# Splitting every second weight group of an input projection one group ahead, from buffers of its own, and holding the first down weights ready

## The chip, the cores and the metric

The kernel runs on one core of a Trainium2 chip. The metric is the device time of one execution in microseconds (us), lower is better. The chip's engines named here are TensorE (PE, with its weight loads PEld), VectorE (DVE), ScalarE (ACT), GpSimd (POOL) and SyncE (SP), on whose queue all the transfers of this kernel are issued in order.

## The reference

One step of a decoder layer for a prompt of 1024 tokens and a sample group of 8 x 8 tokens, which together are 1088 rows of width 1024. All matmuls are float32.

```python
h = x + 0.5 * SwiGLU_1(rms(x))                        # w_gate, w_up, w_down, D_FF = 2816
z = rms(h) @ W_in   # -> [q_A | k_A | v_A | q_B | k_B | v_B | gate_A | gate_B], 2048 + 2048 columns
# A: sliding-window attention, 8 q heads / 2 kv heads, window 128, a learned sink per head
# B: dilated attention, 12 q heads in 3 groups (window, dilation) = (128,1), (512,4), (2048,16),
#    4 kv heads; the sample tokens attend to 2048 cached positions (cache_dil_k, cache_dil_v)
h = h + W_out(sigmoid(gate_A) * (o_A @ W_a) + sigmoid(gate_B) * (o_B @ W_b))
h = h + CrossAttn_4heads(rms(h), memory keys / values)
h = h + 0.5 * SwiGLU_2(rms(h))
y = rms_final(h)
```

## The kernel before, in words

Float32 products are made of three matmuls in a rounded format: both operands are split into a high part and the rest (`xh`, `xl`; `whi`, `wlo`), and high x high, high x low and low x high are summed (`mm3`, L319 to L322).

Weights come through the class `Weights` (L50 to L101). `load` (L61) issues a transfer from HBM into a raw buffer, `split` (L69) makes `whi` on ScalarE (L77) and `wlo` on VectorE (L78) in a ring of split buffers, and `prefetch` (L82) runs splits up to `ring` entries and loads up to `ahead` more ones ahead of use, but not past `limit`. `get` takes the next split entry, `done` frees it and prefetches. The main object `ws` has 4 split buffers and 2 raw ones and walks one list, `entries`, through the whole program: down weights of the first FFN (72), the 16 of the input projection, gate weights and so on. An entry is up to 128 x 1024 numbers, 0.5 MB.

The stages are these.

- First FFN: gate and up products by `products` (L403, loop over `j` in 1 .. NJ-1, NJ = 11) with weight buffers of their own, then `down` (L494): three chunks of tokens, for each 8 output blocks `mo` of three entries. Its results go through `xscr`, and are normalized and split into `xh` and `xl` (L719 to L729; `xa` is chunk 0 loaded back at L721).
- Input projection (L804 to L820): four column groups of 512 (`GRP`, L232), for each 9 tiles of tokens with 24 matmuls (L815 to L817) into PSUM banks pS, pf or pO; ScalarE evacuates (`z_out`, L784, L787), POOL applies the rotary embedding (L778 to L782), and SP stores z (`zscr`, L792; `o_dil_k`, `o_dil_v`, L802).
- Decode attention B for the sample tokens (L830 to L984), in pools opened in the middle of the projection's life by `early`: in pool `db`, twice (two halves `p_`), QP is cleared on POOL (L871), 8 key blocks `krb` are loaded into two buffers (L888), transposed on PE (L892), split into KHb and KLb (L316, L317) and multiplied (L320 to L322), then masked (`ttr`, L761) and put through a softmax (L904 to L919); P is transposed (L933) and split. Then 24 value entries (`cache_dil_v`, 0.5 MB each) come through a `Weights` of three raw and three split buffers, one split after the other, with 26 matmuls for each three (L957 to L971).
- Gate units (`gate`, L1099): 24 matmuls each on gate columns of `w_in`, for 16 blocks x 3 token chunks; `tg` (L1111) takes the result. The program puts them between other work as filler.
- Decode attention A, prompt attention, output projection, memory attention, second FFN.

A scheduler orders the instructions of each engine from the tile dependencies, from buffers and their addresses, and from priorities (`early` raises one). Each engine then works its list in order.

Of the kernel before, what the change touches and what calls it, by code (L numbers as in the profile page):

```python
# [27 lines left out]
RAWB = 2  # L28
# [21 lines left out]
class Weights:  # L50
# [3 lines left out]
    def __init__(self, nc, rawp, ringp, entries, ring, ahead, size=1024):  # L54
        self.nc, self.rawp, self.ringp, self.entries = nc, rawp, ringp, entries
        self.ring, self.ahead, self.size = ring, ahead, size
        self.raw, self.parts = {}, {}
        self.n_raw = self.n_split = self.used = self.taken = 0
        self.limit = len(entries)

    def load(self):  # L61
        n = self.n_raw
# [19 lines left out]
    def prefetch(self):  # L82
        total = self.limit
        while self.n_split < min(self.used + self.ring, total):
            self.split()
        while self.n_raw < min(self.n_split + self.ahead, total):
            self.load()

    def get(self, name):
# [15 lines left out]
NJ = MF // 2  # L105
# [85 lines left out]
def trunk(ctx, tc, A, O, dbg=None):  # L191
    nc = tc.nc
# [3 lines left out]
    def pool(name, bufs=1, space=None, side=None):  # L196
        kw = {} if space is None else {"space": space}
        return tc.tile_pool(name=name, bufs=bufs, side=side, reuse_waits="tile", **kw)
# [15 lines left out]
    entries = []  # L214
# [4 lines left out]
    def kview(n):  # L219
        return lambda t: t[:, :].rearrange("p (k c) -> p k c", k=n)  # L220
# [11 lines left out]
    GRP = [(1024, 512), (512, 512), (1536, 512), (0, 512)]  # L232
    ffn_entries("ffn1")
    w_in = A["w_in"].rearrange("(k p) f -> p k f", p=128)
    for gi, (c0, cw) in enumerate(GRP):
        for kk in range(4):
            entries.append((f"in{gi}.{kk}", [(kview(2), w_in[:, 2 * kk:2 * kk + 2, c0:c0 + cw])], 1024))
    gate_entries = []
    for m in range(16):
        gate_entries.append((f"gt{m}", [(kview(8), w_in[:, :, 2048 + m * 128:2048 + (m + 1) * 128])], 1024))  # L240
# [71 lines left out]
    ws = Weights(nc, rawp, ringp, entries, RING, RAWB)  # L312
# [38 lines left out]
    def norm_stats(psp, ss, j0=0, j1=9):  # L351
        finish_rstd(rcol[:, j0:j1], col_sums(psp, ss, range(j0, j1)), j1 - j0)
# [50 lines left out]
    def products(ops, quads, psA, tp, vp, hook):  # L403

        def bank(tag):
            return psA.tile([128, 512], F32, name="p" + tag, tag=tag, bufs=2)

        def rhs(s, nm):  # L410
            return [a[:, :].rearrange("p (k c) -> p k c", k=4) for a in ops.t[s, nm]]

        def mms(p, w, x, first, last):
            wh, wl = (a.rearrange("p (k f) -> p k f", k=4) for a in w)
            for k in range(4):
                PE.matmul(p, wh[:, k], x[0][:, k], start=first and k == 0, stop=False, skip_group_check=True)  # L416
                PE.matmul(p, wh[:, k], x[1][:, k], start=False, stop=False, skip_group_check=True)  # L417
                PE.matmul(p, wl[:, k], x[0][:, k], start=False, stop=last and k == 3, skip_group_check=True)  # L418

        def out(j, s, v):  # L420
            SP.dma_start(out=hscr[j][s][:, :, :].rearrange("p q c -> p (q c)"), in_=v)

        def new(p, nm):
            return p.tile([128, 4 * H], F32, name=nm, tag=nm, bufs=2)


        w0 = {}
        for s in range(2):
            t, v = new(tp, "tg"), new(vp, "tv")
            pairs = [((0, g), (2, g)) for g in range(2)] + [((1, g), (3, g)) for g in range(2)]  # L430
            if s == 0:
                groups = [(0, 0), (0, 1), (2, 0), (2, 1), (1, 0), (1, 1), (3, 0), (3, 1)]
            else:
                groups = [(0, 0), (1, 0), (0, 1), (1, 1), (2, 0), (3, 0), (2, 1), (3, 1)]
            for n, (c, g) in enumerate(groups):
                b, a1, a2, b1, b2 = PLAIN[c]
                for a in (a1, a2):
                    if (g, a) not in w0:
                        w0[g, a] = quads.get(a)
                p = bank(b)[:, :H]  # L440
                mms(p, w0[g, a1], rhs(s, b1), True, False)
                mms(p, w0[g, a2], rhs(s, b2), False, True)
                cs = slice(c * H, (c + 1) * H)
                if g == 0:
                    S.activation(t[:, cs], p, AF.Silu)
                else:
                    V.tensor_tensor(v[:, cs], t[:, cs], p, op=ALU.mult)
                if s and n % 2:
                    quads.done(2)
                hook(s, n)  # L450
            out(0, s, v)


        for j in range(1, NJ):
            ts = [new(tp, "tg") for _ in range(2)]
            for g in range(2):
                vs = ts if g == 0 else [new(vp, "tv") for _ in range(2)]
                ps = {}
                for i, (b, a, nm) in enumerate(PROD):
                    w = quads.get(a)  # L460
                    for s in range(2):
                        first = (b, s) not in ps
                        if first:
                            ps[b, s] = bank(b)[:, :H]
                        mms(ps[b, s], w, rhs(s, nm), first, True)
                    for s in range(2):
                        p, t = ps[b, s], ts[s]
                        c11, c12, c21, c22 = (vs[s][:, c * H:(c + 1) * H] for c in range(4))
                        if i == 0:
                            S.activation(c22, p, AF.Copy)  # L470
                        elif i == 1:
                            V.tensor_tensor(c12, c22, p, op=ALU.add)
                        elif i == 2:
                            if g == 0:
                                S.activation(c11, p, AF.Silu)
                            else:
                                V.tensor_tensor(c11, t[:, 0:H], p, op=ALU.mult)
                        elif i == 3:
                            V.tensor_tensor(c21, c22, p, op=ALU.add)
                        elif i == 4:  # L480
                            V.tensor_tensor(c22, c21, p, op=ALU.add)
                        elif i == 5:
                            V.tensor_tensor(c21, c21, p, op=ALU.subtract)
                        else:
                            V.tensor_tensor(c12, c12, p, op=ALU.add)
                            o = slice(H, 4 * H)
                            if g == 0:
                                S.activation(vs[s][:, o], vs[s][:, o], AF.Silu)
                            else:
                                V.tensor_tensor(vs[s][:, o], t[:, o], vs[s][:, o], op=ALU.mult)  # L490
                                out(j, s, vs[s])
                    quads.done()

    def down(pre, resid, after, stack, stackr):  # L494

# [64 lines left out]
    with ExitStack() as ph:  # L560
# [96 lines left out]
        def hook1(s, n):  # L657
# [37 lines left out]
            if s == 1 and n == 7:  # L695
                ops.split(1, "T3")
                ops.split(1, "T4")

        products(ops, quads, psA, tp, tp, hook1)
        ws.limit = ws.index("ffn2d0.0.0")  # L700
        pq.close()
        sqp = ph.enter_context(pool("sqp0", 1))
# [35 lines left out]
    with ExitStack() as ph:  # L738
# [63 lines left out]
                    SP.dma_start(out=o, in_=z[:rows, j * 256:(j + 1) * 256])  # L802

        p_m1 = tc.cur_priority  # L804
        norm_stats(Stats(), ss)
        for gi in range(4):
            parts = [ws.get(f"in{gi}.{kk}") for kk in range(4)]
            for n, t in enumerate((5, 6, 7, 8, 3, 4, 0, 1, 2)):
                rows = 128 if t < 8 else 64
                p = bank(psS, "pS") if gi == 0 and n % 5 < 3 else bank(psf, "pf") if n % 5 % 2 else bank(pso, "pO")  # L810
                tok = slice(t * 128, t * 128 + rows)
                for k in range(KD):
                    wh, wl = parts[k // 2]
                    cs_ = slice((k % 2) * 512, (k % 2) * 512 + 512)
                    PE.matmul(p[:rows], xh[:, k, tok], wh[:, cs_], start=(k == 0), stop=False)  # L815
                    PE.matmul(p[:rows], xh[:, k, tok], wl[:, cs_], start=False, stop=False)
                    PE.matmul(p[:rows], xl[:, k, tok], wh[:, cs_], start=False, stop=(k == KD - 1))  # L817
                    if n == 8 and k % 2:
                        ws.done()
                z_out(gi, t, rows, p)  # L820
        p_m1e = tc.cur_priority
        bcast_rstd(Stats())
        if stop("proj"):
# [3 lines left out]
        with early(p_m1), ExitStack() as sp_:  # L827
# [21 lines left out]
            with ExitStack() as sb_:  # L849
# [3 lines left out]
                with pool("db") as db:  # L853
                    maskB = db.tile([128, 832], F32, name="maskB")
                    SP.dma_start(out=maskB, in_=A["c_maskb"])
                    for p_ in range(2):
                        pk = bank(pst, "pT")
                        PE.transpose(pk[:, 0:64], zs[:, 1536 + p_ * 128:1664 + p_ * 128], ident[:64, :64])
                        for g in range(3):
                            c0 = 768 + g * 256 + p_ * 128  # L860
# [92 lines left out]
                for b in range(8):  # L953
# [21 lines left out]
                    for p_ in range(2):  # L975
                        c0 = (p_ * 8 + b) * 16
# [371 lines left out]
    with ExitStack() as ph:  # L1348
# [11 lines left out]
        with ExitStack() as p3:  # L1360
# [5 lines left out]
            for c in range(3):  # L1366
                c0, n = CH[c]
# [98 lines left out]
        for c in range(3):  # L1466
# [4 lines left out]
            c0, n = CH[c]  # L1471
# [23 lines left out]
    with ExitStack() as ph:  # L1495
# [20 lines left out]
        for wi, nm in enumerate(("w_mem_k", "w_mem_v")):  # L1516
            parts = [ws.get(f"{nm}{kk}") for kk in range(4)]
# [230 lines left out]
    with ExitStack() as ph:  # L1748
# [38 lines left out]
                ops2.split(1, "T4")  # L1787

        products(ops2, quads, psA, tp, tp, hook2)
        ws.limit = len(entries)  # L1790
        pq.close()
        xqs.close()
# [134 lines left out]
```

## Time and profile before

| | before |
|---|---|
| median of 3 runs | 2630.32 us (2623.37 to 2632.29) |
| profiled execution, time / span | 2627.26 / 2625.5 us |
| busy: PE, DVE, ACT, POOL | 95%, 57%, 40%, 14% |
| mean granted clock of PE | 0.98 |
| input projection, first matmul | 794.29 us |
| third gate unit, first matmul | 1084.62 us |

The profile is one execution. "Busy" is the share of the span; a wait row gives the time that an engine stood idle before an instruction of a line, and whose instruction ended it. A DMA issue stands on SP at the time of its issue, not of its landing. Lines are those of the kernel before; the changed kernel's line numbers are 1 higher from L61 on, 6 higher around the projection's stores and 13 higher behind the projection.

### The profile page before, as it was taken

To read this page: it belongs to the slowest core of one execution; us is meant where nothing else is said; L and a number is where in the kernel's file an instruction comes from. 1 tells how busy PE (TensorE), PEld (TensorE's weight loads), DVE (VectorE), ACT (ScalarE), POOL (GpSimd) and SP (SyncE) were. 2 spreads that over 40 slices of the span, in tenths; PEclk is the share of its full clock that TensorE was granted. 3 is DMA by queue.
4 is the path that set the end of the run, shared out by engine and by line. 5 is a ranking of instruction groups with operands and counts; after the bars stand their busy time and mean duration, and the time that the engine had idled before them with its cause. 6 is when DMAs were issued, how large, how long until landed. Compare 5 with 4: busy or idle time off the path is not lost.

```text
span 2625.5 us, 43436 instructions
## 1 busy us (share of the span) xinstructions
PE 2505.5 (95%) x16981; PEld 2401.8 (91%) x16981; DVE 1488.2 (57%) x3015; ACT 1049.4 (40%) x1890; POOL 361.2 (14%) x453
## 2 busy tenths in 40 slices
PE   5999999999999999899899899999799999999998
PEld 5999999989997787899798899898799999989998
DVE  6755555554334324468677644475865555656543
ACT  6422223244334234357666424364432223234432
POOL 0000000001114722100234232102200000001111
PEclk7999999999999999999899999999899999999999
DMA  6222222297655745533211462525522222257753
GB/s 190 79 87 70 83 70 87 80 277 214 191 156 178 255 154 161 184 94 93 73 59 60 127 221 72 178 77 171 147 80 69 83 70 87 67 183 204 218 159 91
DMA packets 437197, 341.28 MB, mean 130 GB/s; under 512 B 35088, under 2 KB 407424, under 8 KB 436992
## 3 DMA queue, kind: packets, MB, share of 16 engines
q1 hardware_dynamic: 436992, 338.51, 41.9%
q8 instruction: 133, 2.18, 0.3%
q14 instruction: 72, 0.59, 0.1%
HBM read 267.47 MB, written 70.98 MB: 129 GB/s over the span
## 4 chain that ended last, share of the span: by engine, by line
PE 81%; DMA 7%; DVE 5%; ACT 3%; issue 2%; POOL 1%; SPq 1%; POOLq 0%; ACTq 0%; DVEq 0%
PE pd L322 6%; PE pd L321 6%; PE pd L320 6%; PE pX L418 3%; PE pX L416 3%; PE pX L417 3%; PE pY L416 3%; PE pY L418 3%; PE pY L417 3%; PE pZ L418 3%; PE pZ L416 3%; PE pZ L417 3%; PE pb L320 2%; PE pb L321 2%; PE pb L322 2%
## 5 line engine op out<-in xcount | busy, mean ns | idle before, releaser
L78 DVE TENSOR_TENSOR wlo<-wraw,whi 128x1024 fp32r<-128x1024 f32 (+2 forms) x248 | 284.4, 1151 | 293.1 <-ACT whi L77 291.7
L77 ACT ACTIVATE whi<-wraw 128x1024 fp32r<-128x1024 f32 (+2 forms) x248 | 242.8, 982 | 378.7 <-DMA wraw<-ffn_w_down 149.5
L368 POOL TENSOR_TENSOR ss<-ss,sq 128x384 f32<-128x384 f32 (+2 forms) x98 | 127.4, 1300 | 1728.7 <-ACT sq L367 1720.8
L320 PE MATMUL pd<-h,whi 128*128 128x384 f32 (+1 forms) x1056 | 347.0, 330 | 10.2 <-ACT whi L77 6.9
L321 PE MATMUL pd<-h,whi 128*128 128x384 f32 (+1 forms) x1056 | 347.1, 329 | 2.3 <-DVE h L317 2.3
L322 PE MATMUL pd<-h,wlo 128*128 128x384 f32 (+1 forms) x1056 | 347.6, 329 | 1.6 <-DVE wlo L78 1.6
L163 ACT ACTIVATE whi<-rA 128x512 fp32r<-128x512 f32 x256 | 151.9, 625 | 387.0 <-issue 174.7
L320 PEld LDWEIGHTS pd<-h,whi 128*128 128x128 f32 x1056 | 199.5, 189 | 12.4 <-ACT whi L77 7.8
L321 PEld LDWEIGHTS pd<-h,whi 128*128 128x128 f32 x1056 | 199.7, 189 | 3.5 <-DVE h L317 3.5
L322 PEld LDWEIGHTS pd<-h,wlo 128*128 128x128 f32 x1056 | 199.8, 189 | 2.7 <-DVE wlo L78 2.7
L164 DVE TENSOR_TENSOR wlo<-rA,whi 128x512 fp32r<-128x512 f32 x256 | 169.3, 688 | 33.1 <-ACT whi L163 27.7
L320 PE MATMUL pf<-xh,whi 128*128 128x384 f32 (+1 forms) x336 | 114.7, 341 | 6.6 <-DVE tg L1112 6.5
L322 PE MATMUL pf<-xh,wlo 128*128 128x384 f32 (+1 forms) x336 | 113.5, 338 | 0.0
L321 PE MATMUL pf<-xl,whi 128*128 128x384 f32 (+1 forms) x336 | 112.1, 334 | 0.0
L416 PE MATMUL pX<-B11h,whi 128*128 128x272 f32 x352 | 103.0, 293 | 9.5 <-DVE xo L1587 5.9
L418 PE MATMUL pX<-B11h,wlo 128*128 128x272 f32 x352 | 102.6, 291 | 0.0
L417 PE MATMUL pX<-B11l,whi 128*128 128x272 f32 x352 | 102.1, 291 | 0.0
L418 PE MATMUL pX<-B21h,wlo 128*128 128x272 f32 x352 | 101.6, 289 | 0.0
L416 PE MATMUL pX<-B21h,whi 128*128 128x272 f32 x352 | 101.6, 289 | 0.0
L418 PE MATMUL pZ<-B22h,wlo 128*128 128x272 f32 x352 | 101.5, 288 | 0.0
L416 PE MATMUL pZ<-B22h,whi 128*128 128x272 f32 x352 | 101.3, 288 | 0.0
L417 PE MATMUL pX<-B21l,whi 128*128 128x272 f32 x352 | 101.1, 287 | 0.0
(582 smaller groups left out, 7508.3 us busy)
## 6 DMA issues: line engine op xcount, KB each, us to landing
wraw<-ffn_w_down SPq DMA_DIRECT2D x96, 512.0 KB
hscr<-tv SPq DMA_DIRECT2D x44, 544.0 KB
rA<-ffn_w_gate SPq DMA_DIRECT2D x88, 256.0 KB
rA<-ffn_w_up SPq DMA_DIRECT2D x88, 256.0 KB
wraw<-ffn_w_down SPq DMA_DIRECT2D x48, 384.0 KB
hst<-hscr SPq DMA_DIRECT2D x44, 384.0 KB
wraw<-w_in SPq DMA_DIRECT2D x32, 512.0 KB
wraw<-cache_dil_v SPq DMA_DIRECT2D x24, 512.0 KB
```

Of the source, the lines that this page charges most:

```text
L77: self.nc.scalar.activation(hi[:, :w], t[:, :w], AF.Copy)
L78: self.nc.vector.tensor_tensor(lo[:, :w], t[:, :w], _b(hi[:, :w]), op=ALU.subtract)
L163: self.nc.scalar.activation(hi, r[q], AF.Copy)
L164: V.tensor_tensor(lo, r[q], _b(hi), op=ALU.subtract)
L320: PE.matmul(out, lh, rh, start=first, stop=False)
L321: PE.matmul(out, lh, rl, start=False, stop=False)
L322: return PE.matmul(out, ll, rh, start=False, stop=last)
L368: G.tensor_tensor(ss[:, d0:d0 + n], ss[:, d0:d0 + n], q[:, :n], op=ALU.add)
L416: PE.matmul(p, wh[:, k], x[0][:, k], start=first and k == 0, stop=False, skip_group_check=True)
L417: PE.matmul(p, wh[:, k], x[1][:, k], start=False, stop=False, skip_group_check=True)
L418: PE.matmul(p, wl[:, k], x[0][:, k], start=False, stop=last and k == 3, skip_group_check=True)
```

## The change

Two edits. In `products`, at j = NJ - 3, `ws.held` is set to the number of raw buffers and `prefetch` is called, so that the first two down weights may be loaded although `limit` still holds the splits back; `held` is set back to 0 behind the gate and up part. In the input projection the column groups 1 and 3 come from a list `in_entries` of their own, through a `Weights` object `wi` with three raw buffers (pool `iraw`) and a ring of four (`iring`) on the right side of SBUF, whose prefetch is first called behind the second tile of group 0; the pools are closed behind the projection. Groups 0 and 2 still come through `ws`.

```diff
--- before.py
+++ after.py
@@ -57,6 +57,7 @@
         self.raw, self.parts = {}, {}
         self.n_raw = self.n_split = self.used = self.taken = 0
         self.limit = len(entries)
+        self.held = 0
 
     def load(self):
         n = self.n_raw
@@ -83,7 +84,7 @@
         total = self.limit
         while self.n_split < min(self.used + self.ring, total):
             self.split()
-        while self.n_raw < min(self.n_split + self.ahead, total):
+        while self.n_raw < min(self.n_split + self.ahead, total + self.held):
             self.load()
 
     def get(self, name):
@@ -232,9 +233,10 @@
     GRP = [(1024, 512), (512, 512), (1536, 512), (0, 512)]
     ffn_entries("ffn1")
     w_in = A["w_in"].rearrange("(k p) f -> p k f", p=128)
+    in_entries = []
     for gi, (c0, cw) in enumerate(GRP):
         for kk in range(4):
-            entries.append((f"in{gi}.{kk}", [(kview(2), w_in[:, 2 * kk:2 * kk + 2, c0:c0 + cw])], 1024))
+            (in_entries if gi % 2 else entries).append((f"in{gi}.{kk}", [(kview(2), w_in[:, 2 * kk:2 * kk + 2, c0:c0 + cw])], 1024))
     gate_entries = []
     for m in range(16):
         gate_entries.append((f"gt{m}", [(kview(8), w_in[:, :, 2048 + m * 128:2048 + (m + 1) * 128])], 1024))
@@ -490,6 +492,9 @@
                                 V.tensor_tensor(vs[s][:, o], t[:, o], vs[s][:, o], op=ALU.mult)
                                 out(j, s, vs[s])
                     quads.done()
+            if j == NJ - 3:
+                ws.held = RAWB
+                ws.prefetch()
 
     def down(pre, resid, after, stack, stackr):
 
@@ -697,6 +702,7 @@
                 ops.split(1, "T4")
 
         products(ops, quads, psA, tp, tp, hook1)
+        ws.held = 0
         ws.limit = ws.index("ffn2d0.0.0")
         pq.close()
         sqp = ph.enter_context(pool("sqp0", 1))
@@ -802,9 +808,13 @@
                     SP.dma_start(out=o, in_=z[:rows, j * 256:(j + 1) * 256])
 
         p_m1 = tc.cur_priority
+        ix = ExitStack()
+        wi = Weights(nc, ix.enter_context(pool("iraw", 3, side="right")),
+                     ix.enter_context(pool("iring", 4, side="right")), in_entries, 4, 3)
         norm_stats(Stats(), ss)
         for gi in range(4):
-            parts = [ws.get(f"in{gi}.{kk}") for kk in range(4)]
+            wg = wi if gi % 2 else ws
+            parts = [wg.get(f"in{gi}.{kk}") for kk in range(4)]
             for n, t in enumerate((5, 6, 7, 8, 3, 4, 0, 1, 2)):
                 rows = 128 if t < 8 else 64
                 p = bank(psS, "pS") if gi == 0 and n % 5 < 3 else bank(psf, "pf") if n % 5 % 2 else bank(pso, "pO")
@@ -816,8 +826,11 @@
                     PE.matmul(p[:rows], xh[:, k, tok], wl[:, cs_], start=False, stop=False)
                     PE.matmul(p[:rows], xl[:, k, tok], wh[:, cs_], start=False, stop=(k == KD - 1))
                     if n == 8 and k % 2:
-                        ws.done()
+                        wg.done()
                 z_out(gi, t, rows, p)
+                if gi == 0 and n == 1:
+                    wi.prefetch()
+        ix.close()
         p_m1e = tc.cur_priority
         bcast_rstd(Stats())
         if stop("proj"):
@@ -1787,6 +1800,7 @@
                 ops2.split(1, "T4")
 
         products(ops2, quads, psA, tp, tp, hook2)
+        ws.held = 0
         ws.limit = len(entries)
         pq.close()
         xqs.close()
```

In the built programs `iring` takes bytes 114,656 to 147,424 of each partition and `iraw` 147,424 to 159,712. In both programs pool `db` has its krb buffers at 112,896 to 116,992, KHb at 116,992 to 121,088 and KLb at 121,088 to 125,184.

The three places below are where instructions move. Rows are those of the built programs: line, operation, tiles, shape, and how many alike stand in a row.

SyncE's queue in the last third of the first FFN's down part, before (L721 loads `xa`, L708 stores the result of an output block):

```order
L65 DMA wraw<-ffn_w_down 128x6x128
L65 DMA wraw<-ffn_w_down 128x8x128 x2
L721 DMA xa<-xscr_90 128x8x384
L708 DMA xscr_90<-xr 128x256
L708 DMA xscr_90<-xr 128x64
L65 DMA wraw<-ffn_w_down 128x6x128
L65 DMA wraw<-ffn_w_down 128x8x128 x2
L708 DMA xscr_90<-xr 128x384
```

The same place now:

```order
L66 DMA wraw<-ffn_w_down 128x8x128 x2
L727 DMA xa<-xscr_90 128x8x384
L66 DMA wraw<-w_in 128x2x512
L714 DMA xscr_90<-xr 128x256
L714 DMA xscr_90<-xr 128x64
L66 DMA wraw<-w_in 128x2x512
L66 DMA wraw<-ffn_w_down 128x6x128
L66 DMA wraw<-w_in 128x2x512
L66 DMA wraw<-ffn_w_down 128x8x128
L714 DMA xscr_90<-xr 128x384
L66 DMA wraw<-ffn_w_down 128x8x128
```

Three loads of w_in stand among the down weights, behind the load of `xa`. The first two loads of down weights of the whole program stand four rows apart within the first 50 rows of this queue in both programs.

ScalarE at the end of group 0 of the projection, before (`z` rows evacuate a tile each):

```order
L787 ACTIVATE z<-pS,rcol 128x512 x3
L787 ACTIVATE zs<-pf,rcol 64x512
L787 ACTIVATE z<-pO,rcol 128x512
L787 ACTIVATE z<-pS,rcol 128x512 x3
L77 ACTIVATE whi<-wraw 128x1024 x2
L787 ACTIVATE z<-pf,rcol 128x512
L349 ACTIVATE rbc<-pT 128x512 x2
L349 ACTIVATE rbc<-pT 128x128
L77 ACTIVATE whi<-wraw 128x1024 x2
```

The same place now:

```order
L78 ACTIVATE whi<-wraw 128x1024 x3
L793 ACTIVATE z<-pS,rcol 128x512 x3
L78 ACTIVATE whi<-wraw 128x1024
L793 ACTIVATE zs<-pf,rcol 64x512
L793 ACTIVATE z<-pO,rcol 128x512
L793 ACTIVATE z<-pS,rcol 128x512 x3
L78 ACTIVATE whi<-wraw 128x1024 x2
L793 ACTIVATE z<-pf,rcol 128x512
```

The splits of group 1 moved from the end of group 0 to its first tiles, and those of group 2 follow inside group 0 as well.

SyncE's queue in the last group of the projection, before (L888 loads cached keys):

```order
L888 DMA krb<-cache_dil_k 128x4x128 x2
L802 DMA o_dil_v_p<-z 128x256
L792 DMA zscr<-z 128x512
L802 DMA o_dil_k_p<-z 128x256
L888 DMA krb<-cache_dil_k 128x4x128
L65 DMA wraw<-w_in 128x2x512 x2
L802 DMA o_dil_v_p<-z 128x256
L888 DMA krb<-cache_dil_k 128x4x128
L65 DMA wraw<-w_in 128x8x128
L792 DMA zscr<-z 128x512
L888 DMA krb<-cache_dil_k 128x4x128
L802 DMA o_dil_k_p<-z 128x256
```

The same place now, and what follows up to the values:

```order
L808 DMA o_dil_v_p<-z 128x256
L798 DMA zscr<-z 128x512
L808 DMA o_dil_k_p<-z 128x256
L66 DMA wraw<-w_in 128x8x128 x2
L798 DMA zscr<-z 128x512 x7
L868 DMA maskB<-c_maskb 128x832
L901 DMA krb<-cache_dil_k 128x4x128 x2
L798 DMA zscr<-z 128x512
L901 DMA krb<-cache_dil_k 128x4x128 x14
L960 DMA selB<-c_selb 64x32
L66 DMA wraw<-cache_dil_v 128x1024 x24
```

All 16 key loads moved from between the stores of group 2 and 3 to behind them, and the 24 value loads follow in one piece. On PE, in the same way, the matmuls of the decode attention moved from between the projection's to behind its last tile and behind 38 matmuls of the first two gate units; behind the decode attention the two lists of PE are the same.

## Rows read from the trace of the kernel before

**Rows 1.** Busy time, share of the span and instructions of each engine
```profile
PE 2505.5 (95%) x16981; PEld 2401.8 (91%) x16981; DVE 1488.2 (57%) x3015; ACT 1049.4 (40%) x1890; POOL 361.2 (14%) x453
```

**Rows 2.** Timeline of PE: start, us, instruction [idle before, what ended it]
```profile
794.29 0.50 PE L815 MATMUL pS<-whi,xh 128*128 128x512 f32 x1 [1.02 <-ACT xh L727]
...
1084.62 0.63 PE L320 MATMUL pf<-xh,whi 128*128 128x320 f32 x1 [3.64 <-DVE tg L1112]
```

**Rows 3.** Windows: us, busy (x instructions) by engine, granted clock, DMA share, GB/s
```profile
862.00:893.00 31.00, 30.77 (x133) 23.09 (x131) 8.85 (x14) 3.72 (x6) 24.42 (x47) 1.00 0.88 290
...
1018.00:1070.00 52.00, 52.00 (x317) 44.00 (x316) 29.35 (x27) 27.34 (x30) 9.43 (x16) 1.00 0.77 250
1070.00:1085.00 15.00, 8.63 (x49) 6.83 (x49) 6.49 (x10) 4.64 (x8) 2.38 (x3) 0.75 0.36 112
sum 293.00, PE 277.64 PEld 220.85 DVE 114.91 ACT 105.20 POOL 119.00; mean PE 34.71 PEld 27.61 DVE 14.36 ACT 13.15 POOL 14.87
```

**Rows 4.** Waits of PE in 846 to 862 and 893 to 935: us, times, longest
```profile
PE pO L816 <- DVE wlo L78: 5.4, 3, 3.2
PE pO L815 <- ACT whi L77: 0.4, 1, 0.4
...
PE pO L815 <- ACT whi L77: 0.9, 1, 0.9
PE pO L815 <- ACT z L787: 0.7, 1, 0.7
PE pO L816 <- DVE wlo L78: 0.5, 1, 0.5
```

**Rows 5.** Timeline of SP's queue, the first load of down weights
```profile
66.55 0.39 SPq L65 DMA_DIRECT2D wraw<-ffn_w_down  x1
```

**Rows 6.** Timelines of SP and ACT, a down load and its split
```profile
707.65 0.38 SPq L65 DMA_DIRECT2D wraw<-ffn_w_down  x1
...
715.40 0.85 ACT L77 ACTIVATE whi<-wraw 128x768 fp32r<-128x768 f32 x1 [5.94 <-DMA wraw<-ffn_w_down]
```

**Rows 7.** Key load, its transposes, QP's clearing (timelines); a 0.5 MB load (chain)
```profile
953.63 0.55 SPq L888 DMA_DIRECT2D krb<-cache_dil_k  x1
...
959.09 0.62 PE L892 MATMUL pT<-ident,krb 128*128 128x128 f32 x4
...
965.78 4.07 POOL L871 MEMSET QP<- 128x1152 f32 x4 [0.92 <-PE pS L321]
...
1667.03 3.87 DMA wraw<-w_mem_q
```

**Rows 8.** Softmax: timelines of DVE and ACT, and ACT's wait in it
```profile
1001.78 0.69 DVE L761 CUSTOM_DVE_ANT_0 PB<-pS,maskB 128x512 f32<-128x512 f32 x1 [3.98 <-PE pS L322]
...
ACT PT L316 <- PE pT L933: 2.9, 1, 2.9
...
1014.17 1.05 ACT L77 ACTIVATE whi<-wraw 128x1024 fp32r<-128x1024 f32 x1
```

**Rows 9.** Timeline of SP's queue: value loads 4, 7, 10 (same buffer) and 24
```profile
1016.50 0.33 SPq L65 DMA_DIRECT2D wraw<-cache_dil_v  x1
...
1025.60 0.33 SPq L65 DMA_DIRECT2D wraw<-cache_dil_v  x1
...
1031.93 0.33 SPq L65 DMA_DIRECT2D wraw<-cache_dil_v  x1
...
1070.25 0.33 SPq L65 DMA_DIRECT2D wraw<-cache_dil_v  x1
```

**Rows 10.** Chain of waits: two value matmuls, from their start to the next one's
```profile
1055.61 0.12 PE pS L970
...
1078.81 0.21 PE pS L971
```

## The prediction

> **What bounds the kernel now.** I read the page's busy shares first: TensorE (PE) is busy in 95% of the span [rows 1], so a change gains where PE waits and loses where PE is made to wait. Then I took the stretch that the edits touch, from the first matmul of the input projection at 794.29 to the first matmul of the third gate unit at 1084.62 [rows 2]. Behind the decode attention the two programs issue the same work in the same order, so I let a shift of that second mark pass on to the end. The windows show two kinds of work between the marks. Where PE does projection matmuls alone, it is busy in 30.77 of 31.00 us with 133 of them: 31.00 / 133 = 0.233 us each. Where the decode attention's values arrive, PE is also full (52.00 of 52.00 us) while the DMA queues are 77% busy at 250 GB/s: the transfers lie under projection and gate matmuls. In the last 15 us that cover has run out, and PE is busy for only 8.63 [rows 3]. The reader is to see that the decode attention is work at the pace of transfers, and that the projection hides it.
>
> PE's waits at the borders of the column groups are 5.4 + 0.4 in 846 to 862 and 0.9 + 0.5 in 893 to 935, 7.2 us in all, each on a split of w_in; a wait of 0.7 there is for a PSUM bank [rows 4]. That is all the change can save in this stretch.
>
> **The change, part by part.** *First down weights.* The first of the two loads is already issued at 66.55 in the trace of before [rows 5], and the second stands four places behind it on SyncE's queue (SP) in both programs; the scheduler had hoisted them, and it leaves them where they were. Cost 0, gain 0. In FFN2 a few down loads change places with a load of hidden values by one or two rows; a load's own 2.7 us (below) is the most that this can shift, either way, and I take 0.
>
> *Split a group ahead.* ScalarE's splits for groups 1 and 3 now stand among the previous group's evacuations, so the 7.2 us go. The 0.7 us for the bank stays, at three borders: 2.1.
>
> *Three w_in loads in the first FFN.* They now stand on SP right behind the load of xa, in the last third of its down part, ahead of down weights. There the down queue has little slack: a load issued at 707.65 was split at 715.40, after ScalarE had idled 5.94 us for it [rows 6]. Three loads of 0.5 MB more can cost PE nothing, or as much as one load took from issue to use elsewhere, 5.46 [rows 7]. Three of the shared rate below (2.7) would be 8, but they are spread over two mo steps, and some of it falls into slack that is there: I take 2.
>
> *The decode attention moves.* This is the large term. The new ring and its raw buffers lie on addresses that the pool db holds in both programs (krb, KHb and KLb), so the key loads must wait for the last matmuls of group 3. The order shows it: all 16 key loads stand behind the last projection stores on SP, and on PE the decode attention stands behind 36 dense projection tiles and 38 of the 48 matmuls of the first two gate units. What covered its transfers is then used up. I rebuild the stretch.
>
> 1. Dense projection: 794.3 + 36 tiles x 24 matmuls x 0.233 = 201.4, + 2.8 for some 17 small products of the norm's sums (estimate, 0.16 each), + 2.1 for the banks: 1000.6.
> 2. 38 gate matmuls of 320 to 384 columns: 0.164 (52.00 / 317, a mix with small ones [rows 3]) to 0.233 each; I take 0.18: 6.8. To 1007.4. The first keys arrive beneath these.
> 3. Keys: 16 loads in pairs on two buffers. Nothing in before shows a pair with PE bare. A load of 0.5 MB, as large as a pair, took 3.87 us on an otherwise idle stretch, and the transposes that free the buffers 0.62; one load took from 953.63 to 959.09, 5.46, until its transposes ran [rows 7]. Period 3.87 + 0.62 = 4.5, bounds 3.5 (some overlap) and 5.5. Seven periods: 31.5 (24.5 to 38.5). The second half's clearing of QP takes POOL 4.07 [rows 7]; I take 3 between the halves (0 to 6), and 3.5 from the last pair's landing to its last product. To 1045.4.
> 4. Softmax up to the first split of values: 1001.78 to 1014.17 in before, 12.4, of which ScalarE waited 2.9 for a transpose that stood behind PE's other work [rows 8]. With no other work on PE, 12.4 less 2.9 is 9.5, and a little of the value loads' start is hidden: 9 (8.4 to 12.4). To 1054.4.
> 5. Values: 24 loads on three buffers. In before the 4th was issued at 1016.50 and the 24th at 1070.25: 53.75 / 20 = 2.69 each, 8.06 for three. One buffer alone came round in 1031.93 - 1025.60 = 6.33 [rows 9]. Those queues also carried stores and w_in, which are now done, so I take 7.4 for three (6.3 to 8.1): 7 x 7.4 = 51.8. The end was 1084.62 - (1014.17 + 7 x 8.06) = 14.0 behind; I keep it. To 1120.2.
> 6. The 2 us of the first FFN: 1122.2, against 1084.6: **+37.6 us**.
>
> A check from the other side: PE's work in the stretch is 277.64 [rows 3], about 276.6 of it between the marks. They stand 290.3 apart now, so PE idles for 13.7; by steps 1 to 5 they stand 325.9 apart, and it idles for 49.3. The difference, 35.6, and the 2 of step 6 are the sum. Of the work, 276.6 less 201.4, 2.8 and 6.8 leaves 65.6 for the decode attention, in a block of 1120.2 - 1007.4 = 112.8.
>
> **Rivals.** *A, faster.* The block runs at PE's own pace: 65.6, with 2 to begin and 3 between the halves, ends it at 1007.4 + 70.6 = 1078, 6.6 earlier than before: 2621 (2623 with the first FFN's 2). It decides from the point at which a pair of keys lands in the 3 us that PE works on it (1.2 of transposes and some 1.8 of products, an estimate) and three value loads in about 3.1 (26 matmuls of 0.12 [rows 10]). For it speaks only that the queues are otherwise empty in the block; against it the load of 3.87 and the 6.33. "Perfetto Trace Analysis" of the Trainium skill, section Optimization Strategy, says that gaps which repeat on an engine can mean that there are too few buffers for the next tile, so more buffers should close them; by that alone the sum would be -7.2, and rows 4 agree as far as the borders go.
>
> *B, more slowly than forecast.* PE's clock falls in the block. In before the granted clock is 1.00 in all dense windows and 0.75 in the only bare one, 1070 to 1085, where PE had been waiting for values; matmuls there start 0.21 us apart, against 0.12 earlier [rows 3, 10]. That is the lower level (1.2 of 2.4 GHz), and it adds 0.09 to each of 26 x 8 value matmuls, 19 us of PE time; transposes and products of the keys, some 24 us in all, would take up to twice that. Most of this lies beneath transfers, where PE waits anyway; what follows a landing and frees the buffer for the next load does not. I put that at a quarter of the 43 us, about 11: 2676. Step 5's tail already has one such fall in it. "TensorE: Matmul & The Clock Gate" of the Trainium skill, section Loop structure matters more than you think, says that a long DMA wait between matmuls lets PE go cold; by it B would be the main case, and the window of 0.75 agrees.
>
> *C, no change.* Transfers go most of the way to PE's pace: a pair of keys in 3.2 and three values in 4.5 save 7 x 1.3 = 9 and 7 x 2.9 = 20 of my 37.6, which leaves +8: 2635. No row shows a load that fast with PE's work beside it.
>
> That the change doesn't do what it says is true of its first part, and is in the sum.
>
> **How the numbers follow.** The sum's low ends: 7 (keys), 3 (halves), 0.6, 7.7 (values) and 2 (first FFN) below, -20.3; its high ends that can come together: 7, 3, 3.4, 4.9 and 3, +21.3. The profiled execution took 2627.26; plus 37.6 is 2665, and it stands 3.1 below the median of the runs, which the range covers. Range 2645 to 2686; rival B lies inside. Chances: my sum 0.76, B 0.17, A 0.04, C 0.03. A measurement of this kernel can tell 0.3%, 7.9 us, from no change: faster 0.04 (2621 lies just below that bound), same 0.03, slower 0.93.
>
> **What would show it.** Right: no PE waits at the group borders; projection matmuls dense from 794 to about 1001; the first key transposes at 1007 or so; key loads behind the last store of the projection; PE idle for 45 us or so until a mark near 1122. Wrong: key loads issued inside group 2 or 3 (then A, and the addresses do not bind); values landing every 1.5 us or faster (A or C); PE's clock at its lower level through the block and a mark near 1133 (B); ScalarE's waits for down weights near 720 longer by over 5 us.

## The result: slower, with the decode attention laid bare

The changed kernel takes 2672.24 us (median of 5 runs, 2665.71 to 2672.45) against 2630.32 (5 runs, 2623.37 to 2640.11). The ratio is 1.0150, 95% interval 1.0135 to 1.0165: slower by 1.5%. The profiled execution took 2668.64 us, its span is 2666.9: 41.4 more than before's.

The page's first part, after [rows 1]. PE is busy for 25.1 us more with the same 16981 instructions, so the loss does not show as idle time alone:

```profile
PE 2530.6 (95%) x16981; PEld 2423.3 (91%) x16981; DVE 1487.0 (56%) x3015; ACT 1049.9 (39%) x1890; POOL 359.1 (13%) x453
```

The timeline of PE, after [rows 2]: the projection's first and last matmul, the first transposes of keys, and the first matmul of the third gate unit.

```profile
794.11 0.80 PE L825 MATMUL pS<-whi,xh 128*128 128x512 f32 x1 [1.02 <-ACT xh L733]
...
1003.71 0.40 PE L827 MATMUL pf<-whi,xl 128*128 128x512 f32 x1
...
1010.54 0.60 PE L905 MATMUL pT<-ident,krb 128*128 128x128 f32 x4
...
1123.43 0.63 PE L322 MATMUL pf<-xh,whi 128*128 128x320 f32 x1 [3.63 <-DVE tg L1125]
```

The stretch begins 0.2 us earlier than before and ends 38.8 later (1123.43 - 1084.62). Keys begin at 1010.54, when the projection is over. The windows of the two key halves, the values and their tail, after [rows 3], show what PE does in it (us, PE, PEld, DVE, ACT and POOL busy, granted clock, DMA share, GB/s):

```profile
1005.00:1028.00 23.00, 21.51 (x133) 18.67 (x132) 7.07 (x15) 6.05 (x14) 3.11 (x7) 1.00 0.39 115
1028.00:1051.00 23.00, 18.96 (x100) 16.02 (x99) 9.97 (x28) 9.01 (x20) 4.06 (x4) 0.78 0.29 81
1062.00:1112.00 50.00, 38.30 (x205) 31.19 (x205) 26.80 (x24) 23.12 (x24) 0.00 (x0) 0.74 0.70 218
1112.00:1125.00 13.00, 8.60 (x40) 7.80 (x39) 5.06 (x8) 4.27 (x8) 2.38 (x3) 0.63 0.24 74
```

In [rows 3] the values' window has 317 matmuls in 52 us at a clock of 1.00; here it has 205 in 50 us at 0.74. The waits say who sets this pace. PE's waits from 794 to 1000 (us, times, longest), where the splits of [rows 4] are gone and the wait for a bank has grown from 0.7 to 4.4:

```profile
PE pO L825 <- ACT z L793: 4.4, 2, 3.7
```

PE's and ScalarE's waits from 1062 to 1112: PE waits for splits, and ScalarE, which splits, waits 22.0 of 50 us for value loads.

```profile
PE pS L984 <- DVE wlo L79: 6.3, 8, 0.9
```

```profile
ACT whi L78 <- DMA wraw<-cache_dil_v: 22.0, 18, 3.0
```

In the same window SyncE's queue stands for 40.3 us behind the second part of the splits, which frees the raw buffers:

```profile
SPq L66 <- DVE wlo L79: 40.3, 20, 2.8
```

SyncE's queue, after [rows 7, 9]: keys go out in pairs, the 2nd to 5th pair 3.9 to 5.7 us apart, and the 4th and the 24th value load are 48.65 apart, 2.43 each or 7.30 for three.

```profile
1011.17 1.21 SPq L901 DMA_DIRECT2D krb<-cache_dil_k  x2
1016.84 1.21 SPq L901 DMA_DIRECT2D krb<-cache_dil_k  x2
1020.78 1.29 SPq L901 DMA_DIRECT2D krb<-cache_dil_k  x2
1024.73 1.32 SPq L901 DMA_DIRECT2D krb<-cache_dil_k  x2
...
1061.79 0.33 SPq L66 DMA_DIRECT2D wraw<-cache_dil_v  x1
...
1110.44 0.33 SPq L66 DMA_DIRECT2D wraw<-cache_dil_v  x1
```

### The profile page after: what moved, and what is told of

Same layout as the page of the kernel before. It is cut to its first block, busy times and chain, and to the rows that moved or that the text cites. A ratio compares the mean times of both kernels' runs of the same rounds, so it can differ in the third digit from the quotient of the medians.

```text
span 2666.9 us, 43446 instructions
## 1 busy us (share of the span) xinstructions
PE 2530.6 (95%) x16981; PEld 2423.3 (91%) x16981; DVE 1487.0 (56%) x3015; ACT 1049.9 (39%) x1890; POOL 359.1 (13%) x453
## 3 DMA queue, kind: packets, MB, share of 16 engines
q1 hardware_dynamic: 436992, 338.51, 41.4%
```

## Experiments

My theory: the addresses of the new ring push the decode attention behind the projection, and there its loads set its pace. The rivals: the ring's own loads and splits cost the time; or, of the block, PE's lower clock sets the pace (rival B).

**The first edit alone** (`held`, put into the kernel before).

```diff
+            if j == NJ - 3:
+                ws.held = RAWB
+                ws.prefetch()
```

> The kernel before with the first edit alone (held). Every engine's list has the same rows in the same order as before, so my theory expects no change: 2630 within 8 us, the first down load again near 66.5 us. The rival, that the edit lets the down weights in earlier in FFN1 or FFN2 and pays for part of the change, would show a time off by over 8 us.

2630.03 us, ratio to before 1.0006 (0.9994 to 1.0017), and the first down load is issued at 66.91. As expected, this edit makes no difference that the runs can tell, and what follows is the second edit's. The stretch from the projection's first matmul to the mark (the first matmul of the third gate unit) is 291.7 us in this trace against 290.3 in before's, with the same order of work: a difference of 1.4 us between the stretches of two traces can be noise.

**The addresses alone.** The kernel before, with a tile that holds the ring's addresses and does no work but one memset and one copy.

```diff
+        ix = ExitStack()
+        blk = ix.enter_context(pool("blk", side="right")).tile([128, 11264], F32, name="blk")
+        G.memset(blk[:, 0:1], 0.0)
...
                 z_out(gi, t, rows, p)
+                if gi == 3 and n == 8:
+                    S.activation(blk[:, 0:1], p[:, 0:1], AF.Copy)
+        ix.close()
```

> The kernel before with one unused tile on the addresses of the new ring and its raw buffers (114,656 to 159,712), held until the last matmul of the projection; the weights come as before, so the waits at the group borders stay. If the addresses alone push the decode attention behind the projection, the loss is that of the change with the borders' 7 us on top: 2675 to 2682, key transposes from about 1015. If the ring's own work (loads of w_in ahead of others, splits among the evacuations) makes the loss, it stays near 2630 with transposes of keys near 936.

2681.53 us, ratio 1.0194 (1.0179 to 1.0208). The timeline of PE has the keys at 1022 and the mark at 1136:

```profile
1022.13 1.03 PE L898 MATMUL pT<-ident,krb 128*128 128x128 f32 x8
...
1136.20 0.63 PE L320 MATMUL pf<-xh,whi 128*128 128x320 f32 x1 [3.63 <-DVE tg L1118]
```

PE's waits from 794 to 1000 have the borders' splits back:

```profile
PE pO L818 <- ACT whi L77: 5.2, 1, 5.2
PE pO L819 <- DVE wlo L78: 4.1, 2, 2.9
```

No ring, no early split, no early load, and a larger loss: held addresses are enough. The change is 9.3 us faster than this kernel between the medians, so its ring as such does not cost but gains. The change's shorter waits of PE from 794 to 1000 explain 5.6 of it (4.4 against 10.0, without the first matmul's own). The rest is not separated: the tile also holds its addresses a little longer than the ring, up to a copy behind the last tile.

**Group 1 alone in its own ring**, closed before group 2.

```diff
-            (in_entries if gi % 2 else entries).append(...)
+            (in_entries if gi == 1 else entries).append(...)
...
-            wg = wi if gi % 2 else ws
+            wg = wi if gi == 1 else ws
...
-        ix.close()
+            if gi == 1:
+                ix.close()
```

> The change with group 1 alone in the ring of its own, whose pools are closed behind group 1; group 3 comes as before. The decode attention's keys then meet free addresses. My theory: the borders' 7 us are saved and nothing else, 2622 to 2628, with key transposes near 930. If the loss came from splits a group ahead or from the three w_in loads in the first FFN, about half of it or more stays: 2645 to 2672.

2622.05 us (6 runs, 2616.45 to 2625.82), ratio 0.9966 (0.9953 to 0.9979): faster than before by 0.34%, 7.3 us between the medians. In the trace the stretch is 4.9 us shorter (795.24 to 1080.70): the borders' 7.2 us are gone, and 3.1 of them come back as longer waits for banks. So the median's 7.3 should not be read as the borders' 7.2. The timeline of PE has keys and mark near their places of before:

```profile
932.19 0.98 PE L906 MATMUL pT<-ident,krb 128*128 128x128 f32 x7
...
1080.70 0.64 PE L322 MATMUL pf<-xh,whi 128*128 128x320 f32 x1 [3.64 <-DVE tg L1126]
```

PE's waits from 794 to 1000, behind the first matmul's own, are for banks alone:

```profile
PE pO L825 <- ACT z L793: 2.5, 1, 2.5
PE pf L825 <- ACT z L793: 1.3, 1, 1.3
```

The three early w_in loads and group 1's early splits are in this kernel too, so they are not what costs.

**The tile made smaller.** The larger tile also lies over PB, which the softmax writes; this one lies over PB, but no more over the keys' buffers.

```diff
-        blk = ix.enter_context(pool("blk", side="right")).tile([128, 11264], F32, name="blk")
+        blk = ix.enter_context(pool("blk", side="right")).tile([128, 8576], F32, name="blk")
```

> The kernel before with the unused tile of the blocker run made 10.5 KB smaller, so that it ends above the key buffers (125,408 to 159,712) and lies only over what the softmax writes (PB). If it is the 10 KB over krb, KHb and KLb that push the keys behind the projection, the keys (38 us in the change's trace) are hidden again, while the softmax and the values (8 and 64 us) still wait for the projection's end: 2640 to 2655, key transposes near 936. If any tile held that long does the harm, the time stays near the 2681 of the larger one.

2659.58 us, ratio 1.0117 (1.0102 to 1.0133), above what I expected. The timeline of PE:

```profile
940.26 0.98 PE L898 MATMUL pT<-ident,krb 128*128 128x128 f32 x7
...
1046.17 0.60 PE L898 MATMUL pT<-ident,krb 128*128 128x128 f32 x4
...
1119.29 0.63 PE L320 MATMUL pf<-xh,whi 128*128 128x320 f32 x1 [3.64 <-DVE tg L1118]
```

The keys begin at 940 again, so it was the 10.5 KB over their buffers that held them. But of the larger tile's loss only 16.9 us come back at the mark (1136.20 to 1119.29), not the 38 I counted: the last keys still run at 1046. VectorE's first write to PB, for the first half's softmax, shows what else is held. It comes at 1030.72, against 966.85 in before, and what it waits for is the copy that ends the tile's life:

```profile
1030.72 0.69 DVE L761 CUSTOM_DVE_ANT_0 PB<-pS,maskB 128x512 f32<-128x512 f32 x1 [1.39 <-ACT blk L825]
```

So PB's addresses hold back the first softmax as the key buffers' addresses hold back the keys. That the second half's products then wait for PSUM banks is my reading of the code, not shown. The stretch is 324.8 us here, 342.2 with the larger tile and 290.3 before: 34.5 of the 51.8 us of the larger tile stay without the key buffers' 10.5 KB, with the last keys, the softmax and the values behind the projection.

**Four key buffers for two**, in the changed kernel.

```diff
-                            kr = db.tile([128, 4, 128], F32, name="krb", tag="krb", bufs=2)
+                            kr = db.tile([128, 4, 128], F32, name="krb", tag="krb", bufs=4)
```

> The changed kernel with four key buffers for two. In its trace a pair of keys goes round in 3.9 us in the first half (3.2 from issue to landing, then the transposes free the buffers) and in 4.4 to 8.7 in the second. If the two buffers set that pace, PE's own work on a pair (3 us at full clock) sets it now, and 6 to 12 us of the loss come back: 2660 to 2666. If PE with its lower clock sets it, the time stays within 3 us of 2672.

2665.43 us, ratio to before 1.0129 (1.0110 to 1.0147), which overlaps with the change's interval. The median lies in the range that I gave for the loads' pace, but the trace does not bear that out: its stretch is shorter by 2.7 us (795.50 to 1122.08, against 794.11 to 1123.43), not by 6 to 12. The windows of the two key halves, up to the second half's softmax, in the changed kernel:

```profile
1010.54:1028.88 18.34, 16.85 (x105) 13.89 (x104) 5.69 (x10) 4.95 (x10) 0.95 (x3) 1.00 0.40 114
1028.88:1051.40 22.52, 18.48 (x97) 15.65 (x97) 9.74 (x27) 8.74 (x19) 3.88 (x4) 0.77 0.30 84
```

And with four buffers:

```profile
1013.33:1028.25 14.92, 14.92 (x106) 13.69 (x104) 5.97 (x10) 5.33 (x10) 0.96 (x3) 1.00 0.48 141
1028.25:1049.86 21.61, 18.15 (x97) 15.47 (x97) 9.88 (x28) 8.46 (x18) 3.88 (x4) 0.76 0.24 71
```

The first half gains 3.4 us and PE is then full; the second gains 0.9. In the changed kernel's trace PE waits for key loads for 1.3 us in all:

```profile
PE pT L905 <- DMA krb<-cache_dil_k: 1.3, 3, 0.9
```

So the key loads set only a little of the pace. I had read the second half's slow pairs as transfers, and mostly they are not. PE is busy for 18.48 of 22.52 us there at a clock of 0.77, so its lower clock may well lengthen that half; no run tests it.

**Four raw buffers for values for three**, in the changed kernel.

```diff
-                vs = Weights(nc, sb_.enter_context(pool("vraw", 3, side="right")),
-                             sb_.enter_context(pool("vring", 3, side="right")), dec_entries, 3, 3)
+                vs = Weights(nc, sb_.enter_context(pool("vraw", 4, side="right")),
+                             sb_.enter_context(pool("vring", 3, side="right")), dec_entries, 3, 4)
...
-                    ob = dc.tile([64, 256], F32, name="obB", tag="obB", bufs=2)
+                    ob = dc.tile([64, 256], F32, name="obB", tag="obB", bufs=1)
```

> The changed kernel with four raw buffers for values for three (and one buffer for obB for two, to make room). In its trace a raw buffer goes round in 7.0 us: 4.7 from issue to landing, 1.06 and 1.23 for the two parts of the split. If that loop sets the pace, three loads take 3/4 of 7.0 = 5.3, bounded by PE's 26 matmuls of 0.21 = 5.5 at the lower clock: 7 x 1.5 = 10 us come back, 2659 to 2664. If PE's lower clock already sets the pace, the time stays within 3 us of 2672.

2659.49 us, ratio to before 1.0115 (1.0100 to 1.0130): 12.75 us below the change's median, at the lower edge of what I expected. The mark is at 1112.37, 11.1 earlier:

```profile
1112.37 0.64 PE L322 MATMUL pf<-xh,whi 128*128 128x320 f32 x1 [3.64 <-DVE tg L1125]
```

The 4th and the 24th value load (the first row's second and the last) are 1058.68 to 1099.34 apart, 2.03 us each or 6.1 for three, against 7.30:

```profile
1058.21 0.91 SPq L66 DMA_DIRECT2D wraw<-cache_dil_v  x2
...
1099.34 0.33 SPq L66 DMA_DIRECT2D wraw<-cache_dil_v  x1
```

ScalarE's wait for them from 1062 to 1112 falls from 22.0 to 9.1:

```profile
ACT whi L78 <- DMA wraw<-cache_dil_v: 9.1, 11, 2.8
```

PE's work was left as it was, and one more raw buffer brought the values sooner. So in the changed kernel the loop through the raw buffers sets the pace of the values, not PE at its lower clock.

**Fewer and more value matmuls**, in the changed kernel: the first leaves out three of four products with `wl`; the second repeats products into a bank that is not read.

```diff
-                        PE.matmul(oo, l, wl[:, r_ * 256:(r_ + 1) * 256], start=False, stop=False)
+                        if r_ == 3:
+                            PE.matmul(oo, l, wl[:, r_ * 256:(r_ + 1) * 256], start=False, stop=False)
```

```diff
                         PE.matmul(oo, l, wl[:, r_ * 256:(r_ + 1) * 256], start=False, stop=False)
+                        PE.matmul(pd[:64, 0:256], l, wh[:, 0:256], start=(r_ == 0), stop=(r_ == 3))
```

(and alike for the other 16 of the 24 entries; the second kernel adds one matmul per pair, 12 for each three loads, so 38 in place of the 50 that its expectation counts.)

> The changed kernel with three of four products of the values' low parts left out, so 17 value matmuls for each three loads instead of 26. If the loop through the raw buffers sets the pace, the values take as long as before, 2668 to 2673. If PE at its lower clock sets it, 9 x 0.21 = 1.9 us go for each three: 8 x 1.9 = 15, 2657.

> The changed kernel with each value matmul on high parts done once more into a bank that nobody reads, and once more again for the low part's place: 24 more matmuls of 256 columns for each 26. At the lower clock PE then has 50 x 0.21 = 10.5 us of work for each three loads, more than their 7.0, and the time goes to about 2700. If the fuller PE gets its upper clock, 50 x 0.12 = 6.0 stays under 7.0 and the time stays within 4 us of 2672: then it is the loads, not the clock, that set the block.

2664.57 us (ratio to before 1.0132, 1.0117 to 1.0147) and 2670.45 (1.0155, 1.0140 to 1.0170). The window 1062 to 1112 of the first and of the second:

```profile
1062.00:1112.00 50.00, 40.68 (x151) 27.88 (x151) 27.96 (x25) 23.71 (x26) 0.00 (x0) 0.50 0.71 221
```

```profile
1062.00:1112.00 50.00, 42.40 (x278) 36.76 (x277) 25.67 (x23) 22.12 (x24) 0.00 (x0) 0.82 0.66 209
```

With fewer matmuls the granted clock falls to 0.50, and the 4th and 24th value load are 46.9 us apart instead of 48.65; with more it is 0.82, and they are 50.9 apart. If PE had set the pace, I counted 15 us for 9 matmuls fewer for each three, and 12 more at 0.21 would have made 38 x 0.21 = 8.0 for each three, 0.7 above the 7.30.

Neither run decides it. In the first one's trace the stretch is only 1.8 us shorter, but PE did not have less to do in time: it is busy for 40.68 of the 50 us with 151 matmuls, and for 38.30 with 205 in the changed kernel, since the lower clock took back what the fewer matmuls gave. Its median is 7.7 us below the change's and outside both of my forecasts; the two intervals overlap, and I have no cause for the difference. The second kernel adds less work than I had counted, and its 20 loads took 2.3 us longer. That the loop sets the pace rests on the run with four raw buffers and on the waits of SyncE's queue and ScalarE.

**Group 1 alone and four raw buffers**, the two edits that gained, together.

> Group 1 alone in a ring of its own, closed behind it, and four raw buffers for values for three (one for obB for two). In the kernel before the values run under projection and gate matmuls except for the last 15 us, where PE is busy for 8.6. A shorter loop through the raw buffers can only gain there: 0 to 5 us below the 2622 of group 1 alone, 2617 to 2622. If the faster loads take bandwidth or ScalarE's time from the projection, it is slower, 2623 to 2628.

2619.47 us (5 runs, 2615.55 to 2620.44), ratio 0.9964 (0.9951 to 0.9976). Faster than before and than the change; the interval does not tell it from group 1 alone, though its mark is at 1073.66, from 794.00, which makes the stretch 5.8 us shorter than that of group 1 alone.

## Why the prediction was right

The forecast was 2665 (2645 to 2686), the result is 2672.24. Step by step:

- *First edit, 0*: 2630.03 alone, no difference.
- *Borders*: the 7.2 us are gone, but the bank wait is 4.4 and not 2.1. The mechanism was right, what was late next was under-sized.
- *Three w_in loads, +2*: the stretch begins at 794.11 against 794.29, so -0.2. ScalarE's waits for down weights from 700 to 735 grow from 18.9 to 21.8 us, but PE waits for nothing from 700 to 794 in either trace: slack ahead of the projection took it.
- *Dense part and gates*: keys forecast at 1007.4, measured 1010.54; 2.3 of these 3.1 us are the banks.
- *What is held*: the sum named only the key buffers' addresses. They do hold the keys, but the smaller tile shows that PB's addresses are held too: with the key buffers free, 34.5 of 51.8 us of loss stay.
- *Keys, 38.0*: from 1010.54 to the start of the second half's softmax at 1051.40, 40.9. The sum is near, its mechanism was not: I had seven equal periods of load and transposes. The first half's pairs go round in 3.9, not 4.5, and the second half takes longer (22.5 against 18.3) though four buffers shorten it by only 0.9: what sets it is not the transfers, and stays open.
- *Softmax, 9*: 1051.40 to 1059.46 is 8.1.

The starts of the softmax and of the values' first split, timelines of VectorE and ScalarE after [rows 8]:

```profile
1051.40 0.69 DVE L767 CUSTOM_DVE_ANT_0 PB<-pS,maskB 128x512 f32<-128x512 f32 x1 [1.05 <-PE pS L324]
...
1059.46 1.05 ACT L78 ACTIVATE whi<-wraw 128x1024 fp32r<-128x1024 f32 x1
```

- *Values, 7.4 for three and 14.0 behind them*: 7.30, and 1123.43 - (1059.46 + 7 x 7.30) = 12.9.
- *Sum*: the mark was forecast at 1122.2 and is at 1123.43. That is in part luck: the dense part and the keys came 6.0 us longer than forecast, the softmax, the values and the first FFN 4.7 shorter. The profiled time rose by 41.4 where the mark rose by 38.8; the 2.6 behind it I had set to 0.
- *Idle time*: I forecast that PE idles for 49.3 us between the marks instead of 13.7. The windows between the marks, of before and of the changed kernel, give 14.3 (290.33 less 275.99) and 33.3 (329.32 less 296.06):

```profile
794.29:1084.62 290.33, 275.99 (x1370) 219.28 (x1370) 112.94 (x186) 102.73 (x167) 119.00 (x213) 0.99 0.58 190
```

```profile
794.11:1123.43 329.32, 296.06 (x1370) 236.44 (x1371) 113.34 (x186) 102.70 (x167) 117.32 (x213) 0.91 0.51 163
```

So only 18.9 of the 39.0 us show as idle time, and 20.1 as the same 1370 matmuls taking longer, at a mean clock of 0.91 in place of 0.99. The forecast of the time held all the same, since the terms for the values were paced by loads.

Rival A, the block at PE's own pace, fell by the 22.0 us for which ScalarE waits for values. Rival B is the instructive one: its condition came true, since the clock is at 0.63 to 0.78 in the second half of the keys, among the values and in their tail, and PE's busy time rose by 25.1 us with the same matmuls. Among the values its price was not paid: 26 matmuls at 0.21 are 5.5 us for each three loads, under the 7.3 of the loop, and a fourth raw buffer brought three loads to 6.1 with the clock at 0.77. For the second half of the keys and for the tail no run tests it. The trace agrees with "TensorE: Matmul & The Clock Gate" of the Trainium skill, section Loop structure matters more than you think, that a long wait for transfers between matmuls lets PE go cold: its clock is 0.74 among the values. What "Perfetto Trace Analysis" of the Trainium skill, section Optimization Strategy, says, that repeated gaps can mean too few buffers, held at the borders (7.2 us) and among the values (11.1 us at the mark); the price of the further buffers, in addresses, is what this change missed.

## What to carry to other kernels

Ask of every new buffer whose addresses it takes and until when: a ring and its raw buffers on addresses of the next stage's key buffers and softmax, held until the last tile, undid an overlap of two stages that was worth over 40 us to save 7. Free the buffers when their last user is done: the same idea for group 1 alone, with its buffers freed behind that group, gains 0.3%. Where work at the pace of transfers is bare, look for the loop through its buffers (issue, landing, split, free) before looking at the engine that uses the data.

## What was not expected

PE's busy share stays at 95% through a loss of 42 us: matmuls at a lower granted clock count as busy, so a stretch that waits for data can look full. The windows' granted clock (1.00 in the dense part, 0.74 among the values) and the count of matmuls (205 in 50 us, against 317 in 52) show it; the busy time does not. And with fewer matmuls the clock fell further, from 0.74 to 0.50, while with more it rose to 0.82, and 20 value loads took 46.9 to 50.9 us in all three.
